# Interleaving the two groups of a turn in memory: row pitch 128 KiB in place of 64 KiB, in a log-softmax backward kernel

## Chip, cores, metric

One core of a Trainium2 chip, the others idle. The metric is the time of one execution on the device in microseconds.

## The reference

```python
# y, dy: float32 [8, 1024, 8192]
def reference(y, dy):
    softmax_x = np.exp(y)
    sum_dy = np.sum(dy, axis=-1, keepdims=True)
    return (dy - softmax_x * sum_dy).astype(np.float32)
```

Each row of 8192 numbers needs its own sum of `dy`, and then one product and one subtraction for each element. Two tensors of 268 MB are read and one is written: 805 MB.

## The kernel before

The 8192 rows are cut into 32 groups of 256. In a group each of the 128 partitions holds R = 2 whole rows, W = 16,384 numbers or 64 KiB, which are neighbours in memory. Sixteen turns take two groups each (j = 0 and 1); the first turn is written out, the other fifteen are a loop with branches. The three lines that the change touches say where a group lies:

```python
    R = 2
    W = R * D                  # 16384 floats = 64 KiB for each partition
    G = N // (P * R)           # 32 groups
    ...
    y_v = y.flatten_outer_dims().rearrange("(h j p r) d -> h j p (r d)", j=2, p=P, r=R)
    dy_v = dy.flatten_outer_dims().rearrange("(h j p r) d -> h j p (r d)", j=2, p=P, r=R)
    out_v = out.flatten_outer_dims().rearrange("(h j p r) d -> h j p (r d)", j=2, p=P, r=R)
    ...
    def load_dy(h, j):
        nc.sync.dma_start(out=x_ts[j][:], in_=dy_v[h, j])
    def load_y(h, j, at):
        nc.sync.dma_start(out=y_t[:, at : at + W], in_=y_v[h, j])
    def store(h, j, lo, hi):
        return nc.sync.dma_start(out=out_v[h, j][:, lo:hi], in_=x_ts[j][:, lo:hi])
    ...
    def two_groups(h, boundary, early):
        load_dy(h, 0)
        load_y(h, 0, SHIFT)
        boundary()
        early()
        sums(0)
        compute(0, SHIFT, EXP_A, (IN_PSUM, IN_PSUM + Q))
        load_dy(h, 1)
        boundary()
        early()
        sums(1)
        load_y(h, 1, 0)
        compute(1, 0, EXP_B, ())
        boundary()
        stores = [store(h, 0, 0, W), store(h, 1, 0, D), store(h, 1, D, W)]
        # each pair of the three stores is declared independent

    two_groups(0, lambda: None, lambda: None)
    with tc.For_i(1, G // 2, 1, iteration_sync="staggered") as h:
        two_groups(h, tc.stage_boundary, done_early)
```

`sums` adds up the rows of `dy` (one on VectorE, one on ScalarE); `compute` takes exp on ScalarE piece by piece and combines on VectorE. All transfers are issued from the SP engine: seven in a turn, five of 8 MiB and two of 4 MiB. The two `y` buffers overlap, so SP must often wait before it may issue a load.

## Time and profile before

| | before |
|---|---|
| time, median (lowest to highest) | 1867.83 us (1867.74 to 1868.14) |
| busy: DMA queue / VectorE / ScalarE | 99.8% / 46% / 37% |
| moved | 805.3 MB in 14,336 data packets |
| rate over the span / inside turns | 432 / 434 GB/s |

A packet is what one DMA engine moves at a time; here it is one partition's row of 64 KiB (or of 32 KiB in the two half stores). If 16 engines have a packet in hand at every moment, the run's length is the sum of the packets' times divided by 16, and nothing else.

The view is the DMA queue's own waits of the kernel before; the columns are us in total, times, longest us.

```profile
SPq L68 <- DVE x L97: 610.5, 33, 30.5
SPq L131 <- DMA y_t<-in_y_dram: 568.3, 15, 37.9
SPq L131 <- DMA out_dram<-x: 226.4, 28, 10.0
```

L68 is the store, L131 and L97 are the loop's boundaries and the combining on VectorE. SP waits through most of the run, and still the DMA engines are never short of work, because what SP issued earlier is still being moved.

### The profile page before, as it was taken

The numbers are of one execution on the slowest core, as the hardware profiler recorded it, in microseconds if no ns is written. First come the engines' busy times: TensorE is split into PE (matmuls) and PEld (weight loads), VectorE is DVE, ScalarE is ACT, GpSimd is POOL, SyncE is SP. The second block draws the span as 40 slices with busy tenths as digits, with TensorE's granted clock in tenths as the row PEclk, the third lists the DMA queues.
The fourth block names the chain that finished last, engine by engine and source line by source line (L and its number), as shares of the span: only waits on it lengthen the run. The fifth ranks groups of instructions, "written<-read, shape, count | busy, mean of one in ns | idle before, by whom it ended". The sixth has DMA issues, their size and how long they took to land.

```text
span 1866.1 us, 2175 instructions
## 1 busy us (share of the span) xinstructions
DVE 861.9 (46%) x288; ACT 689.0 (37%) x273; POOL 0.2 (0%) x4
## 2 busy tenths in 40 slices
DVE  2717427173271732717327173271633716337163
ACT  2606326053260532605326053260533605335153
POOL 0000000000000000000000000000000000000000
DMA  9999999999999999999999999999999999999998
GB/s 427 427 427 427 431 445 427 430 445 423 433 444 433 427 438 438 427 434 441 428 429 443 431 428 434 438 430 433 437 433 428 435 438 431 438 434 427 440 435 368
DMA packets 16129, 805.32 MB, mean 432 GB/s; under 512 B 1792, under 2 KB 1792, under 8 KB 1792
## 3 DMA queue, kind: packets, MB, share of 16 engines
q1 hardware_dynamic: 16128, 805.31, 99.8%
q14 instruction: 1, 0.01, 0.0%
HBM read 536.87 MB, written 268.44 MB: 432 GB/s over the span
## 4 chain that ended last, share of the span: by engine, by line
DMA 51%; DVE 15%; ACT 11%; another core or an unknown queue 10%; issue 5%; SPq 1%; ACTq 0%
DMA x<-in_dy_dram 29%; DMA y_t<-in_y_dram 22%; DVE x L97 15%; ACT x L76 6%; ACT y_t L93 5%; SPq L68 0%; SPq L131 0%; ACTq L93 0%; SPq L65 0%; SPq L62 0%; SPq L158 0%; ACTq L131 0%; ACTq L76 0%
## 5 line engine op out<-in xcount | busy, mean ns | idle before, releaser
L97 DVE SCALAR_TENSOR_TENSOR x<-y_t,stats,x 128x1024 f32<-128x1024 f32 (+2 forms) x192 | 511.1, 2704 | 389.7 <-ACT y_t L93 389.2
L73 DVE TENSOR_REDUCE stats<-x 128x1 f32<-128x8192 f32 x32 | 278.0, 8686 | 594.4 <-DMA x<-in_dy_dram 591.1
L93 ACT ACTIVATE y_t<-y_t 128x3072 f32<-128x3072 f32 (+6 forms) x176 | 403.7, 2362 | 392.2 <-DMA y_t<-in_y_dram 392.2
L76 ACT ACTIVATE x<-x 128x8192 f32<-128x8192 f32 x32 | 225.0, 7030 | 758.1 <-DMA x<-in_dy_dram 758.1
L97 DVE SCALAR_TENSOR_TENSOR x<-e_t,stats,x 128x2048 f32<-128x2048 f32 x32 | 73.7, 2344 | 0.0
L93 ACT ACTIVATE e_t<-y_t 128x2048 f32<-128x2048 f32 x32 | 58.5, 1858 | 0.0
L76 ACT ACTIVATION_READ_ACCUMULATOR x<-x 128x1 f32 x32 | 6.0, 186 | 0.0
L77 DVE TENSOR_SCALAR stats<-stats 128x1 f32<-128x1 f32 x32 | 4.6, 144 | 0.0
L76 ACT ACT_TABLE_LOAD x1 | 1.3, 1283 | 0.7 <-PEq L147 0.7
L147 POOL MEMSET const-bfloat16-1.0<- 128x1 bf16 x1 | 0.1, 101 | 0.0
L147 POOL MEMSET const-uint8-127<- 128x1 uint8 x1 | 0.1, 101 | 0.0
L147 POOL MEMSET const-float32-0.0<- 128x1 f32 x1 | 0.1, 98 | 0.2 <-issue 0.2
L147 POOL MEMSET const-float32-1.0<- 128x1 f32 x1 | 0.1, 98 | 0.0
## 6 DMA issues: line engine op xcount, KB each, us to landing
out_dram<-x SPq DMA_DIRECT2D x32, 4096.0 KB, 18.2
x<-in_dy_dram SPq DMA_DIRECT2D x32, 47.0
y_t<-in_y_dram SPq DMA_DIRECT2D x32, 34.6
out_dram<-x SPq DMA_DIRECT2D x16, 37.6
```

Of the source, the lines that this page charges most:

```text
L73: nc.vector.tensor_reduce(out=stats[:, c : c + 1], in_=x[:, :D], axis=mybir.AxisListType.X, op=ALU.add, negate=True)
L76: nc.scalar.activation(x[:, D:], x[:, D:], COPY, accum_out=stats[:, c + 2 : c + 3])
L77: nc.vector.tensor_scalar(out=stats[:, c + 1 : c + 2], in0=stats[:, c + 2 : c + 3], scalar1=-1.0, scalar2=None, op0=ALU.mult,)
L93: nc.scalar.activation(e_ap, y_t[:, at + b : at + e], EXP)
L97: nc.vector.scalar_tensor_tensor(out=x[:, lo:hi], in0=e_ap[:, lo - b : hi - b], scalar=stats[:, 4 * j + r : 4 * j + r + 1], in1=x[:, lo:hi ...
L147: nc = _bacc.Bacc("TRN2", target_bir_lowering=False, num_devices=1)
```

## The change

The intent: let each partition take 128 KiB of neighbouring memory in a turn, half of it in each of the two groups, so that a turn covers one block of 16 MiB without jumps between its groups. It is done by the order of two letters.

```diff
-    y_v = y.flatten_outer_dims().rearrange("(h j p r) d -> h j p (r d)", j=2, p=P, r=R)
-    dy_v = dy.flatten_outer_dims().rearrange("(h j p r) d -> h j p (r d)", j=2, p=P, r=R)
-    out_v = out.flatten_outer_dims().rearrange("(h j p r) d -> h j p (r d)", j=2, p=P, r=R)
+    y_v = y.flatten_outer_dims().rearrange("(h p j r) d -> h j p (r d)", j=2, p=P, r=R)
+    dy_v = dy.flatten_outer_dims().rearrange("(h p j r) d -> h j p (r d)", j=2, p=P, r=R)
+    out_v = out.flatten_outer_dims().rearrange("(h p j r) d -> h j p (r d)", j=2, p=P, r=R)
```

A single transfer thereby loses something: its 8 MiB were one block, and are now 128 pieces of 64 KiB with gaps of 64 KiB. The distance from one partition's row to the next, the row pitch, doubles to 128 KiB.

## The prediction

> **What bounds the kernel now.** I began with the page's rows of DMA and of the engines, because the change touches nothing but addresses in HBM.
>
> ```profile
> span 1866.1 us, 2175 instructions
> DVE 861.9 (46%) x288; ACT 689.0 (37%) x273; POOL 0.2 (0%) x4
> DMA  9999999999999999999999999999999999999998
> DMA packets 16129, 805.32 MB, mean 432 GB/s; under 512 B 1792, under 2 KB 1792, under 8 KB 1792
> q1 hardware_dynamic: 16128, 805.31, 99.8%
> ```
>
> The compute engines are idle more than half of the time; the 16 DMA engines are never below 90% in any of the 40 slices but the last, and the packets of the one queue fill 99.8% of 16 engines' span. 99.8% of 1866.1 us is 1862.4 us for each engine. So the time is the sum of packet times, plus about 4 us. The chain of waits (51% DMA, then DVE, ACT and 10% unknown) would suggest that a third of the span hangs on compute. That can't be used here: it follows semaphores and doesn't see that the queue works on other transfers meanwhile.
>
> Next: is the rate steady, or is there a stage with something to win? I asked for four pairs of loop turns, each 233 us long, since one turn takes 116.5 us (the SP engine's timeline has the first load of a turn at 567.81 and the y load after it at 568.41, the next turn's at 684.27 and 684.87).
>
> ```profile
> 336.00:569.00 233.00, 107.75 (x36) 85.97 (x34) 0.00 (x0) 1.00 1.00 434
> 569.00:802.00 233.00, 107.75 (x36) 85.96 (x34) 0.00 (x0) 1.00 1.00 434
> 802.00:1035.00 233.00, 107.75 (x36) 85.97 (x34) 0.00 (x0) 1.00 1.00 434
> 1035.00:1268.00 233.00, 107.75 (x36) 85.96 (x34) 0.00 (x0) 1.00 1.00 433
> ```
>
> The last two columns are the DMA share, 1.00, and GB/s. Every turn runs at 433 to 434 GB/s. That is 27.1 GB/s for an engine, or 2.42 us for a row of 64 KiB (65,536 / 27.1e9). The trace's packet records, read one by one, agree: 10,240 packets of 65,536 bytes with a median of 2418 ns, the 10th percentile 2418 too and the 90th 2422; 4,096 packets of 32,768 bytes with a median of 1213 ns, 90th percentile 1213; 1,792 of 4 bytes, 9 ns each. So a packet is one partition's row, and load or store makes no difference to it: they all sit on one value. 111 rows take over 2440 ns; 30 of those are in the first loads and the first store, where rows took up to 3640 ns. All 111 together cost 2.5 us of each engine's time.
>
> The sum: 10,240 x 2.4228 (their mean) / 16 = 1550.6; 4,096 x 1.2133 / 16 = 310.6; 1,792 x 0.009 / 16 = 1.0; together 1862.2 us. Outside them the trace has 1.8 us before the first packet and 1.9 us after the last, so no gap is left in the middle.
>
> **What the Trainium skill says.** "DMA: Bandwidth & Descriptors", section "Where 436 GB/s comes from", puts the ceiling of 16 ports of 32 B at 850 MHz at 435.2 GB/s. The trace agrees: 434 GB/s in steady state, and 2,048 beats of 32 B at 850 MHz are 2409 ns, against the 2418 ns measured. The limit is thus the engines' own port, not the memory behind it. The "HBM Reference", section "Specifications (TRN2)", gives about 716 GB/s for the stack that two cores share; only one core runs here, so by that page memory has slack. No run yet tests how much. The one entry that speaks of the change is in the first page's section "Latency and other measured facts", "HBM row pitch at large powers of two": copies of 128-partition tiles ran at 207 GB/s per direction with a row pitch of 512 KiB, 164 at 2 MiB, 103 at 4 MiB, and 214 at full rate. The pitch here goes from 64 KiB to 128 KiB, below everything in that list. The trace of before can't show it for 128 KiB, but it has a small relative of the case, below.
>
> **The change part by part.** Removed: nothing. Added: no instruction, no byte, no packet, no wait. What moves is the address of a row. Before, group j of turn h was a contiguous block of 8 MiB, in which partition p had 64 KiB at p x 64 KiB. After, the two groups of a turn share 16 MiB: partition p owns 128 KiB, group 0 takes the first half of it and group 1 the second. Rows stay 64 KiB in SBUF and in HBM; only the HBM pitch doubles.
>
> - *Packets.* A row was already its own packet although the whole 8 MiB was contiguous: 128 packets for a transfer, (10,240 + 4,096) for 80 full and 32 half transfers. So contiguity across rows buys nothing today, and losing it takes nothing: 14,336 data packets of the same sizes.
> - *Time of a packet.* The half stores are the evidence in hand. They write 32 KiB of each row at a pitch of 64 KiB, so they already leave a gap as long as the run, just as every transfer will after the change. Their packet takes 1213 ns, twice that is 2426, 8 ns over the full row, and the short packet's fixed cost explains that. A gap of half the pitch costs no more than 0.3%, and with rows of the old size nothing at all is expected: 2418 ns. Engines work on rows some partitions apart, so their streams sit a few hundred KiB apart already now and keep a constant rate.
> - *Issue on SP.* The instruction costs 332 to 424 ns for the loads of dy now. Suppose the pattern with a gap costs 0.1 us more in each of 112 transfers: 11 us of SP, none of it on the path, since the queue has work in front of it.
>
> ```profile
> L68 SPq DMA_DIRECT2D out_dram<-x x48: 332/355/361, 62.1 to 1846.1; - x48
> out_dram<-x SPq DMA_DIRECT2D x32, 4096.0 KB, 18.2
> x<-in_dy_dram SPq DMA_DIRECT2D x32, 47.0
> y_t<-in_y_dram SPq DMA_DIRECT2D x32, 34.6
> out_dram<-x SPq DMA_DIRECT2D x16, 37.6
> ```
>
> (first the stores' issue on SP, ns min/median/max, half and whole alike; then median us from issue to landing.) 8 MiB at 434 GB/s takes 19.3 us and 4 MiB 9.7. A load lands 34.6 or 47.0 us after its issue and a half store 18.2 us, so each stood behind 8.5 us or more of other transfers. That is the slack of the queue against a late issue.
>
> - *Order and waits.* The stores of a turn are declared independent of each other in both versions, the inputs are never written, and the stage boundaries stand where they stood. I expect the same instructions in the same order.
>
> The sum of the changes: 0 us on the path; the run stays at 1868 us. A fraction of a microsecond either way may come from the slow first rows, where other addresses are touched first.
>
> **The rivals.**
>
> *Memory aliasing takes over as the bound.* Power-of-two pitches put lock-stepped streams onto fewer channels. For it: the page's row, and the fact that all packets take the same 2418 ns, so that engines do run in step. Against it: 128 KiB is a quarter of the smallest pitch listed, where the loss was only 3% (207 of 214), and now, with strides of 64 KiB and multiples, only one row in a hundred is over 2453 ns. If the whole loss of the 512 KiB pitch came (my estimate from that page), the time would be 1868 x 214 / 207 = 1931 us; a tenth of it would make 1874.
>
> *Rows are cut in two by the descriptor generator,* because the HBM side is no longer one contiguous block. The half packets give the price: 24,576 packets x 1.2133 / 16 = 1863.6 in place of (10,240 x 2.418 + 4,096 x 1.2133) / 16 = 1858.1, so 5.5 us more, 1873 us; cut into smaller packets, more. Against it: the SBUF side already forces a packet to a row.
>
> *Better locality makes it faster.* A turn's two groups are neighbours, which may have been the intent: [...]a better start. For it: some rows are slow, mostly at the start. Against it: removing every slow row wins 2.5 us (0.13%). Even at the page's 435.2 GB/s the data takes 805.31 / 435.2 = 1850.4 us, and with the 3.7 us of start and end 1854 us, 0.7% below now. Faster by 2% would be under 1830 us, which the ports can't do.
>
> *A wait or dependency appears,* for instance if overlapping address ranges of the two groups of out make a store wait for another one. All pairs within a turn are declared free, and between turns the boundary waits anyway. If stores did wait for each other, the queue would drain two times in each of 16 turns; at about 2 us each (the 1.9 us that the span goes on after the last packet, as an estimate of what a landing takes to be known) that is some 64 us, 1932 us. I give it 2%.
>
> **Range and chances.** Nothing on the path changes, and the runs of before lie within 0.4 us. The lower end is cut by the ports, so 1863 us leaves room for the slow rows and half of the fixed cost. Upward stand the mild forms of aliasing and of cut rows: 1882 us covers a quarter of the page's 3%. Slower by 2% (over 1905 us) needs a mean row of 2.47 us; aliasing 3%, a dependency 2%, together 5%. Faster by 2%: under 1%.
>
> **What would show it right or wrong.** In the changed profile the packets should number 16,129 with the same sizes, queue q1 stand at 99.8%, the windows of two turns at 433 to 434 GB/s, and the median row at 2418 ns. Cut rows would show as more packets and a lower mean. Aliasing would show as rows above 2418 ns with the DMA share still 1.00 and fewer GB/s, all over the run or in stores or loads alone. A new wait would show as a DMA share under 1.00 inside a turn, and in the DMA queue's own waits as a store that waits for out. A slower SP would show in longer issues, and matters only if the share falls too. I'd be wrong outright if 16 streams at the doubled distance meet in the same part of memory: the half stores are the only evidence here that they don't.

## The result, and the profile after

The changed kernel takes 1867.62 us (median of four, 1867.23 to 1867.83), against 1867.78 us (1867.41 to 1868.14) of the kernel before. The ratio is 0.9999, with a 95% interval of 0.9982 to 1.0016: the same.

The page of the changed kernel, its lines on span, engines, packets and queue (the page's rows that the prediction showed of before):

```profile
span 1866.0 us, 2175 instructions
DVE 861.9 (46%) x288; ACT 689.0 (37%) x273; POOL 0.2 (0%) x4
DMA packets 16130, 805.32 MB, mean 432 GB/s; under 512 B 1793, under 2 KB 1793, under 8 KB 1793
q1 hardware_dynamic: 16128, 805.31, 99.8%
```

The kernel's own queue moved exactly as many packets as before, in the same share of the span. (The one packet more belongs to the fetching of instructions, on another queue.) The windows of two turns each, with DMA share and GB/s in the last two columns:

```profile
336.00:569.00 233.00, 107.75 (x36) 85.96 (x34) 0.00 (x0) 1.00 1.00 433
569.00:802.00 233.00, 107.75 (x36) 85.97 (x34) 0.00 (x0) 1.00 1.00 434
802.00:1035.00 233.00, 107.75 (x36) 85.96 (x34) 0.00 (x0) 1.00 1.00 434
1035.00:1268.00 233.00, 107.75 (x36) 85.97 (x34) 0.00 (x0) 1.00 1.00 434
```

These are the rates of before. In the trace's packet records the median row takes 2418 ns (2418 before), the 90th percentile is 2422 (2422), the mean 2422.9 (2422.8); 100 rows take over 2440 ns (111 before), and they cost 2.4 us of each engine's time (2.5). The sum over all packets is 1862.2 us an engine in both kernels.

The stores' issue on SP in the changed kernel (ns, min/median/max), from the view of the tile x; then, from its page, the loads' median us from issue to landing:

```profile
L69 SPq DMA_DIRECT2D out_dram<-x x48: 332/356/362, 61.9 to 1846.0; - x48
```

```profile
x<-in_dy_dram SPq DMA_DIRECT2D x32, 47.2
y_t<-in_y_dram SPq DMA_DIRECT2D x32, 34.7
```

The issue costs a median of 356 ns in place of 355. The 0.1 us that I had allowed for a pattern with gaps wasn't needed. The DMA queue's own waits of the changed kernel (every line number is one higher):

```profile
SPq L69 <- DVE x L98: 610.4, 33, 30.8
SPq L132 <- DMA y_t<-in_y_dram: 568.9, 15, 38.1
SPq L132 <- DMA out_dram<-x: 225.2, 28, 9.8
```

The same waits, as often, and as long within 1.2 us. No line has a store that waits for another one. So the two traces are alike in every row that the change could have moved. What they can't tell is why the address pattern costs nothing: is the memory indifferent to it, is it hidden behind compute, or is there a limit that this pitch merely doesn't reach? The experiments ask that.

### The profile page after: what moved, and what is told of

It is laid out like the page before. It is cut to its first block, busy times and chain, and to the rows that moved or that the text cites. A ratio compares the mean times of both kernels' runs of the same rounds, so it can differ in the third digit from the quotient of the medians.

```text
span 1866.0 us, 2175 instructions
## 1 busy us (share of the span) xinstructions
DVE 861.9 (46%) x288; ACT 689.0 (37%) x273; POOL 0.2 (0%) x4
## 4 chain that ended last, share of the span: by engine, by line
DMA 51%; DVE 15%; ACT 11%; another core or an unknown queue 10%; issue 5%; SPq 1%; ACTq 0%
DMA x<-in_dy_dram 29%; DMA y_t<-in_y_dram 22%; DVE x L98 15%; ACT x L77 6%; ACT y_t L94 5%; SPq L69 0%; SPq L132 0%; ACTq L94 0%; SPq L63 0%; SPq L66 0%; SPq L159 0%; ACTq L132 0%; ACTq L77 0%
```

## The experiments

Theory: the run is the sum of packet times; a packet's time is set by the DMA engine's port, as long as the memory behind it can follow. Rivals: compute hides the effect; neighbouring memory does matter, and 64 KiB of it is just enough; the pitch does matter, and 128 KiB lies below a threshold (the prediction calls this aliasing: rows that lie a large power of two apart slow each other down). Edits are against the changed kernel. Kernels are compared only within the same rounds.

### Compute cut to an eighth

```diff
+            e = b + (e - b) // 8                     # exp and combining
-  in_=x[:, :D]                                       # sum of dy, first row
+  in_=x[:, :1024]
-  nc.scalar.activation(x[:, D:], x[:, D:], COPY, ...)   # sum, second row
+  nc.scalar.activation(x[:, D : D + 1024], x[:, D : D + 1024], COPY, ...)
```

> Wrong result on purpose: the changed kernel with each compute instruction cut to about an eighth of its columns, all transfers left. Theory (the sum of packet times is the time, compute is hidden): 1866 us, within 3 us, DMA share 1.00, median row 2418 ns. Rival (the chain of waits is right that compute carries a quarter or more of the span, and the change of addresses was hidden behind compute): the busy time of VectorE and ScalarE falls by some 85%, and the time falls by 100 us or more.

Measured: 1867.42 us, ratio 1.0001 (0.9984 to 1.0017). Its engines' row on the page, then its windows of two turns each:

```profile
DVE 141.8 (8%) x272; ACT 115.5 (6%) x273; POOL 0.2 (0%) x4
```

```profile
336.00:569.00 233.00, 17.73 (x34) 14.28 (x34) 0.00 (x0) 1.00 1.00 433
569.00:802.00 233.00, 17.73 (x34) 14.28 (x34) 0.00 (x0) 1.00 1.00 433
```

Over 1290 us of engine work is gone and the time stands still. The rival falls: compute hid no cost of the changed addresses, and the chain of waits, which gives DVE and ACT a quarter of the span, names no cost here. (The result passed as correct although it was meant to be wrong. With these inputs the term that compute subtracts has a norm of 1.9% of that of dy, computed from the first of the eight batches, so the comparison hardly sees it. For the other kernels it still tells whether rows go where they belong: the kernels below that misplace them have an error of 1.41, and the one that leaves part of out unwritten has "nan".)

### Rows cut to 32 KiB, 4 MiB apart

```diff
-  "(h p j r) d -> h j p (r d)"
+  "(h j r p) d -> h j p r d"      # all three tensors; tiles viewed as p r d
```

> Correct result. A partition's 64 KiB are taken as two rows of 32 KiB that lie 4 MiB apart in memory, so every packet is cut to 32 KiB and even a row's neighbourhood is gone. Theory (contiguity beyond a packet is worth nothing, a packet has a small fixed cost): 24,576 packets of 32,768 bytes at 1213 ns, 1863.6 us of packets, with the slow rows and ends some 1872 us, 0.2 to 0.4% over before. Rival (neighbouring memory matters, the 64 KiB runs of both versions are just long enough): rows above 1213 ns, 1890 us or more.

Measured: 1871.69 us, correct, ratio 1.0023 (1.0006 to 1.0040). Packets and queue on its page:

```profile
DMA packets 26370, 805.32 MB, mean 431 GB/s; under 512 B 1793, under 2 KB 1793, under 8 KB 1793
q1 hardware_dynamic: 26368, 805.31, 99.9%
```

10,240 packets more, as many as there were full rows, and 4.3 us more time, as the theory expected. The packet records have a median of 1213 ns and a mean of 1215.7, so the packets sum to 24,576 x 1.2157 / 16 = 1867.4 us an engine, 6.2 us over the changed kernel's 1861.2. The span grew by 3.9 us only; the stretch at its end in which fewer than 16 packets are in hand is 0.7 us shorter (3.9 in place of 4.6), and the rest of the difference I can't place. This is near the price of rival "rows cut in two" in the prediction (5.5 us), and it is the price of packets, not of distance: two rows of a partition lay 4 MiB apart, and within about 1 us that cost nothing. But a transfer as a whole is still one block of 8 MiB here: the rows of neighbouring partitions touch. So this kernel doesn't show that a packet needs no neighbours at all. The last kernel below (all three tensors at 31 x 64 KiB) does: there no two rows of a transfer touch, and in its packet records the rows of 64 KiB have a median of 2418 ns and the half rows, 32 KiB each, one of 1213 ns with a mean of 1213.3, as before.

### Larger pitches: 1 MiB and 2 MiB

```diff
-  "(h p j r) d -> h j p (r d)"     # pitch 128 KiB
+  "(j p h r) d -> h j p (r d)"     # first kernel: 1 MiB
+  "(p h j r) d -> h j p (r d)"     # second kernel: 2 MiB
```

> Correct result. The same transfers with a row pitch of 1 MiB in place of 128 KiB. Theory with slack (memory far from its limit whatever the addresses): 1868 us, rows at 2418 ns. Rival (pitches of large powers of two alias; the Trainium skill's row has 207 of 214 GB/s at 512 KiB and 164 at 2 MiB, so between these at 1 MiB): 1930 to 2430 us, rows at 2.5 to 3.1 us with the DMA share still 1.00; then 128 KiB was free because it lies below the limit, not because addresses never matter.

> Correct result. Row pitch of 2 MiB, the largest that a partition-outermost layout of these tensors has. Theory with slack: 1868 us. Rival (aliasing as in the skill's row, 164 of 214 GB/s): 1867 x 214 / 164 = 2436 us, rows at about 3.15 us.

Measured: 1914.44 us at 1 MiB, ratio 1.0253 (1.0236 to 1.0270), and 1971.49 us at 2 MiB, ratio 1.0554 (1.0524 to 1.0585), both correct. The theory with unlimited slack falls. The rival's direction holds, but its size doesn't: 1 MiB stays below the 1930 us that were its least, and 2 MiB costs 5.5% in place of 30%.

Where does the time go? One turn of the 2 MiB kernel, cut at its transfers, in order: load of y (j = 0), load of dy (j = 1), load of y (j = 1), the first two stores, the third store (4 MiB), and the next turn's first load of dy.

```profile
1007.00:1026.00 19.00, 8.75 (x2) 7.12 (x2) 0.00 (x0) 1.00 1.00 435
1026.00:1045.00 19.00, 12.86 (x7) 14.42 (x7) 0.00 (x0) 1.00 1.01 435
1045.00:1065.00 20.00, 14.25 (x4) 7.12 (x2) 0.00 (x0) 1.00 1.00 426
1065.00:1095.00 30.00, 18.02 (x6) 14.32 (x6) 0.00 (x0) 1.00 0.97 418
1095.00:1109.00 14.00, 0.00 (x0) 0.00 (x0) 0.00 (x0) 1.00 1.05 316
1109.00:1129.00 20.00, 0.00 (x0) 0.00 (x0) 0.00 (x0) 1.00 1.00 410
```

And the last two of these stretches for the changed kernel (128 KiB) in a turn at nearly the same time:

```profile
1038.00:1047.00 9.00, 0.00 (x0) 0.00 (x0) 0.00 (x0) 1.00 1.05 451
1047.00:1067.00 20.00, 0.00 (x0) 0.00 (x0) 0.00 (x0) 1.00 1.00 431
```

The engines are busy all the time in both (a share near 1.00; a little over it in a short window, as a packet counts where it starts). But in the third store the 2 MiB kernel moves 316 GB/s, and in the load behind it 410; the other stretches run at full rate or close to it. In the packet records, counted off in order of start (full and half rows apart), 64 KiB of this third store takes 3.43 us in the mean and a row of the load behind it 2.61 us, while 64 KiB in the other stretches takes 2.42 to 2.46 us. Summed over the run, rows over their usual 2418 or 1213 ns cost 103 us of each engine's time; 48 of them are in the third stores and 31 in the loads of dy (j = 0), 27 of these behind a third store. (The expectation for the loads alone, below, says "almost wholly"; it is nearly three quarters.) So a busy DMA engine can mean two things, and only the GB/s beside it tells full rate from slow rows. The change at hand has nothing of the sort in the windows above.

### Between: 128, 256 and 512 KiB with the turns written out

Pitches between 128 KiB and 1 MiB can't be addressed with one loop variable, so these three have no loop.

```diff
-    two_groups(0, lambda: None, lambda: None)
-    with tc.For_i(1, G // 2, 1, iteration_sync="staggered") as h:
-        two_groups(h, tc.stage_boundary, done_early)
+    for h in range(G // 2):
+        two_groups(h, lambda: None, lambda: None)
...
+  "(b e f p j r) d -> b e f j p (r d)"   # 128 KiB, the control
+  "(b e p f j r) d -> b e f j p (r d)"   # 256 KiB
+  "(b p e f j r) d -> b e f j p (r d)"   # 512 KiB
```

> Correct result. The changed layout (pitch 128 KiB) with the 16 turns written out and no loop: the control for the next two, because pitches of 256 and 512 KiB can't be written with one loop variable. It also tests whether the loop has any part in the result. Both theories: 1866 to 1869 us, median row 2418 ns.

> Correct result. Pitch of 256 KiB, otherwise as the control. Theory (a threshold above 128 KiB, well away from the change): within 2 us of the control. Rival (a loss that grows steadily with the pitch and is already there at 128 KiB, only too small to see; 2.5% at 1 MiB halved for each halving of the pitch would be 0.6% at 256 KiB): 1879 us.

> Correct result. Pitch of 512 KiB, where the Trainium skill's row has 207 of 214 GB/s. By that page: 1867 x 214 / 207 = 1930 us. By the measured 2.5% at 1 MiB, halved: 1890 us. With a threshold between 512 KiB and 1 MiB: 1868 us.

| row pitch | time, us | over the kernel before of the same rounds |
|---|---|---|
| 64 KiB (before) | 1867.78 | |
| 128 KiB (the change) | 1867.62 | ratio 0.9999 |
| 128 KiB, no loop | 1867.48 | 0.9998 (0.9981 to 1.0015) |
| 256 KiB, no loop | 1867.06 | 0.9998 (0.9981 to 1.0015) |
| 512 KiB, no loop | 1874.79 | 1.0042 (1.0026 to 1.0059) |
| 1 MiB | 1914.44 | 1.0253 |
| 2 MiB | 1971.49 | 1.0554 |

All are correct. The loop has no part in the result. The first loss that can be seen is at 512 KiB. The slope that halves with each halving of the pitch is out, since 256 KiB should then have cost 0.6% and its interval ends at 0.15%. A loss smaller than that can't be excluded by the times; the packet records show none, as rows over 2440 ns cost 3.4 us of each engine's time at 256 KiB, 3.6 in the control and 8.3 at 512 KiB. At 512 KiB none of the three expected times came (1930, 1890, 1868 us): there is a loss, but a small one. It came mostly in the first turns of the profiled run; two of the windows there:

```profile
336.00:569.00 233.00, 105.80 (x36) 85.97 (x34) 0.00 (x0) 1.00 1.00 430
569.00:802.00 233.00, 107.67 (x37) 85.97 (x34) 0.00 (x0) 1.00 1.00 433
```

The change thus stood two doublings below the first pitch with a measurable loss.

### Loads alone and stores alone at 2 MiB

```diff
-  y_v, dy_v: "(h p j r) d -> h j p (r d)"
+  y_v, dy_v: "(p h j r) d -> h j p (r d)"     # first kernel: the loads only
-  out_v: "(h p j r) d -> h j p (r d)"
+  out_v: "(p h j r) d -> h j p (r d)"         # second kernel: the stores only
```

> Wrong result on purpose: loads of y and dy with a pitch of 2 MiB, stores with the 128 KiB of the change. With both at 2 MiB, the loss of 104 us sat almost wholly in the second half store of a turn and in the load of dy behind it. If reads alone set it: some 60 us of the loss stay, and the store is as slow as it was. If the meeting of reads and writes of like pitch sets it: less than 20 us stay. If writes alone set it: rows of the loads at 2418 ns and 1870 us.

> Wrong result on purpose: the mirror of the loads at 2 MiB. Stores at a pitch of 2 MiB, loads at the 128 KiB of the change. Loads alone took 35 us of the 104 us. If the two sides add: 1867 + 69 = 1936 us, with the loss in the second half store. If the rest came from like pitches meeting on both sides: 1875 us or less.

Both give a wrong result: rows come from one place and go to another. Loads alone: 1902.53 us, ratio 1.0186 (1.0169 to 1.0203), 35 us over the kernel before. Stores alone: 1948.82 us, 1.0428 (1.0410 to 1.0445), 81 us over. Together 116 us, against 104 us with both at 2 MiB. So the two sides add, roughly, and a meeting of like pitches on both sides isn't needed. With the loads alone, 64 KiB of the half stores is back at 2432 ns in the mean; with the stores alone it stays at 2816 ns, as with both (2815). I had expected 60 us of the loads if they set the loss by themselves; they give little more than half of that. A third of the bytes, the stores, give two thirds of the loss.

### Is it the power of two, or the spread?

A pitch of 2 MiB also spreads a transfer over 128 separate places. A pitch of 31 x 64 KiB does that just as much and isn't a power of two. With 32 groups at this pitch the tensor would be overrun, so 31 are used and one is taken twice; the group is h + 15 j, and a control has the same order at 2 MiB.

```diff
-  y_v = y...rearrange("(h p j r) d -> h j p (r d)", j=2, p=P, r=R);   in_=y_v[h, j]
+  y_v = y...[: P * 31 * R, :].rearrange("(p g r) d -> g p (r d)", p=P, r=R);   in_=y_v[15 * j :][h]
# dy the same; the control has 32 in place of 31; the third kernel does it to out as well
```

> Wrong result on purpose: control for the next. Loads at a pitch of 2 MiB (32 x 64 KiB), with group h + 15 j in place of 2 h + j, so that the next can use the same order. As the loads at 2 MiB before: 1895 to 1910 us.

> Wrong result on purpose: as the control, but with a pitch of 31 x 64 KiB, 2 MiB less 64 KiB. A partition's rows lie as far apart and a transfer touches as many separate regions. If it is the power of two that makes rows slow (streams meeting in the same part of memory): 1867 to 1872 us, first load back to rows of 2.5 us in the mean. If it is the spread over many regions of memory: as the control, 1895 us or more.

> Wrong result on purpose: all three tensors at the pitch of 31 x 64 KiB (31 groups, one taken twice). If the power of two is the cause: 1867 to 1872 us against the 1971 us of 2 MiB. If the spread is: 1950 us or more.

Measured: control 1897.83 us, ratio 1.0166 (1.0149 to 1.0183); loads at 31 x 64 KiB 1868.03 us, ratio 1.0001 (0.9984 to 1.0017); all three tensors at 31 x 64 KiB 1867.71 us, ratio 0.9998 (0.9982 to 1.0015). Their outputs are wrong, which doesn't matter for the times. The last kernel's first turn and two pairs of later ones, and then the first turn of the 2 MiB kernel:

```profile
0.00:102.00 102.00, 53.78 (x18) 44.27 (x18) 0.20 (x4) 1.00 0.99 421
336.00:569.00 233.00, 107.74 (x36) 85.96 (x34) 0.00 (x0) 1.00 1.00 433
569.00:802.00 233.00, 107.74 (x36) 85.97 (x34) 0.00 (x0) 1.00 1.00 434
```

```profile
0.00:102.00 102.00, 42.45 (x15) 38.79 (x16) 0.20 (x4) 1.00 0.99 383
```

The first turn's 421 GB/s are the changed kernel's there too. A pitch shorter by one partition's 64 KiB takes the whole loss away: 30 us of the loads, against a control with the same order of groups, and 104 us with all three tensors, where the 2 MiB kernel to compare with took its groups in the plain order. The spread over many places costs nothing; it is the power of two, from 512 KiB up, that goes with slow rows. Only this one other pitch was tried, so how far from a power of two is far enough isn't shown. What in the memory the addresses share at such a pitch, these runs don't show.

No kernel here beats the kernels before and after the change. The best of them differ by less than the intervals, and the packets fill the span to within 4 us.

## Why the prediction was right

**The bound.** "The time is the sum of packet times": shown. An eighth of the compute leaves 1867.42 us, and both kernels' packets sum to 1862.2 us an engine.

**Packets.** The count and sizes of packets stayed as they were, since a row was already its own packet. Losing contiguity beyond it costs nothing at 128 KiB, and the kernel with rows cut to 32 KiB confirms the other half: the cost of cutting is the fixed cost of more packets (4.3 us measured, 5.5 us predicted for that rival). The prediction's reason, that the SBUF side forces a packet to end with a row, wasn't tested: no kernel here has rows longer than 64 KiB, so a greatest size of 64 KiB would look the same.

**Time of a packet.** "2418 ns" in the median after the change, exactly. The half stores, which I took as the only evidence in hand, pointed the right way, though they were weaker than I made them: they have a gap, but their pitch is the 64 KiB of the full rows, so they say nothing of 128 KiB, and the later runs show that gap and distance are not what matters.

**Issue, order and waits.** Unchanged: 356 in place of 355 ns, the same waits in the same number.

**The rival of aliasing.** It is real, and this was the one that could have made the prediction wrong. I gave 3% to it on the Trainium skill's row "HBM row pitch at large powers of two" ("DMA: Bandwidth & Descriptors", section "Latency and other measured facts"), because 128 KiB lay a quarter of the way to its smallest pitch. The runs find the first loss at 512 KiB and none at 256 KiB, so the argument held. But nothing in the trace of before bore on 128 KiB: that it would be free was read off a list that starts at 512 KiB, and to that extent it was luck. The estimate attached to it, 1931 us for the whole loss of 512 KiB, was too large by far: 512 KiB costs 7 us here, not 63. The page's copies went between tensors in HBM in rows of 16 KiB, and these transfers have rows of 64 KiB; whether that is the reason isn't tested.

**A detail that was off.** I put 16 of the slow rows into the first store. Counted off in order of start, they are the last 16 of the 128 rows of the y load ahead of that store, in both kernels (77 us into the span of the changed one). All slow rows together cost 2.4 us, so it didn't matter. What makes the rows slow just there stays open.

**What narrows the loss at 2 MiB.** The third store of a turn suffers and the first two hardly. In the packet records of the 2 MiB kernel its half rows have a mean of 1541 to 1715 ns in the first fifteen turns, where the next turn's loads stand close behind it, and of 1270 ns in the last turn, where no load follows; with the stores alone at 2 MiB it is 1485 to 1705 and 1317 ns. The first two stores of a turn have the third behind them, not a load. So the loss goes mostly with a load close behind a store. That is seen, not shown as a cause: no run moved that load, and with the stores alone the first store was slow too in the first turns (2990 ns a row in the first).

**Two figures of the prediction that were off.** Its lower end, 1863 us, was said to leave room for the slow rows and half of the packets' fixed cost. The packets' 1861.2 us less its 1850.4 us for the data at the port's rate and 2.5 us of slow rows make some 8 us of fixed cost, so the 4.8 us between 1863 and 1867.8 hold the slow rows and less than a third of it. And the chain of waits gives DVE and ACT 26% of the span (15% and 11%), not a third. Neither bore on the 1868 us.

**Locality.** The gain that may have been intended had nowhere to come from. Every full row but a hundred or so already took 2418 to 2440 ns, against the 2409 ns that the prediction worked out for the port.

## What to carry to other kernels

Before judging a change of memory layout, look whether packets change; if each packet keeps its size and already takes about the time that its bytes need at the port, as here, there is nothing to win from neighbourhood beyond the packet. Keep row pitches of large powers of two away: up to 256 KiB they were free here, from 512 KiB they cost, above all in stores, and 64 KiB off the power of two gave all of it back. A DMA share of 1.00 with GB/s below the usual is the mark of slow packets, so read the two together and by stage.

## What the Trainium skill lacked or had wrong

- "DMA: Bandwidth & Descriptors", section "Latency and other measured facts", row "HBM row pitch at large powers of two": the list starts at 512 KiB and gives 207 of 214 GB/s there and 164 at 2 MiB. With rows of 64 KiB in loads and stores, 64 to 256 KiB were free, and the loss in time was 0.4% at 512 KiB, 2.5% at 1 MiB and 5.5% at 2 MiB, where the page's figures would make 3% at 512 KiB and 30% at 2 MiB (an estimate from them). The page's advice to leave the power of two agrees in direction: 31 x 64 KiB ran at 1867.71 us against 1971.49 us. Its own remedy, a pad of a few KiB, wasn't run.
- The same row doesn't part reads from writes: loads alone at 2 MiB cost 35 us, stores alone 81 us, with half as many bytes.
- The same page, section "Where 436 GB/s comes from", says in its warning that for transfers between HBM and SBUF the HBM side (about 358 GB/s) binds. With one core alone these kernels moved 432 GB/s over the span and 434 in a turn. The "HBM Reference", section "Specifications (TRN2)", has this right in kind, with about 425 GB/s for a core that streams alone.
- No page gives a measured fixed cost of a packet this long (the first page has about 3 cycles a packet, in "Why small descriptors are slow (HBM only)", with an example of 256 bytes): 2418 ns for 64 KiB and 1213 ns for 32 KiB lie 8 to 9 ns over the 2409 and 1205 ns that 32 B at 850 MHz make (an estimate from the ceiling in the first page's section "Where 436 GB/s comes from"), and twice 1213 less 2418 is 8 ns too.
